# Two edits to the norms of a two-layer encoder: the first norm's small operations on POOL, the last layer's norm by column halves

## The chip, the cores and the metric

One core of a Trainium2 chip runs the whole program. The metric is the device time of one execution in microseconds (us). The core's engines run side by side, each with its own instruction queue worked off in order: PE (matrix products), DVE (vector operations), ACT (activations, with sums along a row), POOL (further vector operations) and SP, whose queue issues the DMA transfers. An engine waits at the head of its queue for semaphores of other engines.

## The reference

Two layers over 1024 positions of width 1024: a recurrent mixer in the first, windowed attention in the second, each followed by an MLP. Each of the four sub-layers is normed before and after:

```
def rmsnorm(x, g):
    xf = x.astype(jnp.float32)
    y = xf * lax.rsqrt(jnp.mean(xf * xf, axis=-1, keepdims=True) + EPS) * g.astype(jnp.float32)
    return y.astype(x.dtype)
...
        h = h + rmsnorm(m.astype(h.dtype), g[1])
        m = sqrelu_mlp(rmsnorm(h, g[2]), mlp_w1[layer], mlp_w2[layer])
        h = h + rmsnorm(m.astype(h.dtype), g[3])
```

So at the end of a sub-layer stand two norms: that of its output m, added to the residual h, and that of the new h, which feeds the next sub-layer. The last sub-layer has only the first of them.

## The kernel before

All products are split into high and low parts of 32-bit floats, three matmuls for one. A scheduler orders the instructions on each engine from the program's text and its own estimates of their durations; the text gives priority, so one edit can move rows elsewhere.

At the end of a sub-layer the output exists as eight blocks of 128 positions by 1024 columns, `acc[b]`, in SBUF. A block's product is made in two column halves of 512, each in its own bank of PSUM (`g2_block`, matmul at L216). Each half is added into `acc` by DVE (L267 in an output projection, L586 in an MLP) or copied by ACT (L264, blocks 0 to 3 of a projection). Then `add_norm(b)` runs the first norm:

- SP loads the old h into hb (L234).
- POOL multiplies acc by the gain into mg (L236). mg has two buffers in a projection and one in an MLP.
- `rsqrt_neg2` makes the scale r: ACT squares the block and sums along the row (L147; a second row of it reads the sum out into ss), DVE makes the mean plus epsilon (ms, L148), ACT takes the root (L149), DVE the reciprocal y (L150), and two DVE operations refine it: e (L151) and r (L152), a Newton step with a factor of -2 that the gains' factor of -0.5 undoes. All of these but the square are 128x1. In profile and order the tiles ss, ms and sq are called a, m and s.
- DVE makes the new h, hb = mg * r + hb (L238), and SP stores it (L243).

`normed` (L183 to L185) repeats `rsqrt_neg2` on hb, and DVE writes hb * r * g over acc at L185. `turn(b)` transposes the result on PE (L191), ACT copies the high part (L204) and DVE subtracts to the low part xl (L205). The last layer's MLP has no second norm and no transposes; there a rule puts block b's L238 behind the adds of block b + 1.

Four such tails run: the two output projections (at about 470 to 550 us and 1520 to 1590 us of the span), the first MLP (1122 to 1190) and the last (2164 to the end). Behind a projection's tail the first products of the MLP (L413) follow, with many DVE operations that prepare their operands (L402 to L406, L356 to L359, L86).

Of the kernel before, what the change touches and what calls it, by code (L numbers as in the profile page):

```python
# [18 lines left out]
P = 128  # L19
D = 1024  # L20
# [31 lines left out]
def trunk_kernel(ctx, tc, x, norm_g, rec_w_in, rec_conv_w, rec_conv_b, rg_w_r, rg_b_r, rg_w_i,  # L52
# [87 lines left out]
    def rsqrt_neg2(pool, src, tag, junk=None):  # L140
        def small(t):
            return pool.tile([P, 1], F32, tag=tag + t, name=t, bufs=3)

        if junk is None:
            junk = pool.tile([P, D], BF16, tag="junk", name="junk", bufs=1)
        ss, ms, sq, y, e, r = (small(t) for t in "amsyer")
        A.activation(junk, src, AF.Square, accum_out=ss)  # L147
        V.tensor_scalar(ms, ss, 1.0 / D, EPS, op0=ALU.mult, op1=ALU.add)  # L148
        mm_state["sqrt"] = A.activation(sq, ms, AF.Sqrt)  # L149
        V.reciprocal(y, sq)  # L150
        V.scalar_tensor_tensor(e, y, ms[:, 0:1], y, op0=ALU.mult, op1=ALU.mult)  # L151
        V.scalar_tensor_tensor(r, e, -3.0, y, op0=ALU.add, op1=ALU.mult)  # L152
        return r
# [20 lines left out]
                if self.strassen:  # L174
                    self.f[i][sh] = x_tile(f"xf{i}{sh}", F32)

    def load_g(pool, layer, j):
        g = pool.tile([P, D], F32, tag="g", name="g", bufs=2)
        Y.dma_start(g, norm_g[layer, j, :].partition_broadcast(P))
        V.tensor_scalar(g, g, -0.5, None, op0=ALU.mult)  # L180
        return g
# [40 lines left out]
    def make_tail(pool, acc, h_src, h_dst, layer, j_post, nxt, nbuf, mb):  # L222


        g_post = load_g(pool, layer, j_post)
        state = {}
        if nxt is not None:
            state["g"] = load_g(pool, *nxt)
            state["xt"] = Acts(nxt[1] == 2)

        def add_norm(b, after):
            m = acc[b]
            hb = pool.tile([P, D], F32, tag="hb", name="hb", bufs=nbuf)
            Y.dma_start(hb, h_src[b * P:(b + 1) * P, :])  # L234
            mg = pool.tile([P, D], F32, tag="mg", name="mg", bufs=mb)
            G.tensor_tensor(mg, m, g_post, op=ALU.mult)  # L236
            r = rsqrt_neg2(pool, m, "rt")
            ins = V.scalar_tensor_tensor(hb, mg, r[:, 0:1], hb, op0=ALU.mult, op1=ALU.add)  # L238
            if after is not None and nxt is None:
                tc.add_manual_dep(ins.ins, after.ins.name,  # L240
                                  mybir.DependencyInfo(mybir.DependencyClass.NoSync, mybir.DependencyReason.DATA),
                                  reason="evacuate the next block first")
            Y.dma_start(h_dst[b * P:(b + 1) * P, :], hb)  # L243
            if nxt is not None:
                normed(pool, hb, state["g"], m)

        def turn(b):
            if nxt is not None:
                prep(acc[b], state["xt"], b)
        return add_norm, turn, state  # L250
# [58 lines left out]
    def mlp(xt, hgs, layer, h_src, h_dst, nxt, pre):  # L309
# [391 lines left out]
        with phase("mlp2", reuse_waits="tile") as pool:  # L701
            seq, fetch, prep, group, finish = strassen_out(pool)
            tiles = {}
            hids = {j: plain_hid(j, hl_tile(xp, "x")) for j in (0, 1)}
            for j in (0, 1):
                split_in_place(*hids[j])
                tiles[j] = hids[j], plain_w2(j, hl_tile(wp, "w1", bufs=3))
            fetch(0)
            fetch(1)
            acc += [yp.tile([P, D], F32, tag="y", name=f"acc{b}") for b in range(NB)]  # L710
            todo = {1: lambda: prep(0), 3: lambda: prep(1)}
            plain((0, 1), tiles, True, None, lambda b: todo.get(b, lambda: None)())
# [618 lines left out]
```

## Time and profile before

| | us |
|---|---|
| median of 3 runs | 2219.73 (2218.73 to 2221.28) |
| the profiled execution | 2219.73 |
| its span | 2218.0 |
| L236, POOL's product, 32 times | 80.3, mean 2.509 |
| ACT's root, 128x1 (L149, for example at 2210.30) | 0.20 |
| DVE add of a half block (L586), median | 0.684 |
| a store of a half megabyte to out, issue to landing, median | 2.6 |

The span is what the profile's records cover. In the timeline's rows the start and the duration of an instruction stand first, then engine, line, operation and the tiles written and read; in brackets how long its engine was idle before it and what ended the wait. "x2" merges two neighbours of one kind. In the stretches' table the busy times of PE, PEld (the weight load), DVE, ACT and POOL follow the length, each with a count, then PE's granted clock, the DMA engines' busy share and GB/s.

### The profile page before, as it was taken

The page shows a single profiled execution, that of the slowest core. Times are in us where ns is not written, and L with a number is a line of the kernel's source. Part 1 is how long each engine was busy: PE and PEld are TensorE (multiplying, and loading weights), DVE is VectorE, ACT ScalarE, POOL GpSimd, SP SyncE. Part 2 cuts the span into 40 slices and gives each one's busy share as a digit, 9 for nine tenths or more (in the row PEclk, how much of TensorE's full clock was granted, in tenths as well). Part 3 has the DMA queues.
Part 4 walks back from the last instruction along what each step waited for, and adds up shares of the span by engine and source line. Part 5 has one row for each costly group of instructions (what it writes and reads, how often), then busy time and mean ns, then how long its engine had stood idle before and what let it go on. Part 6 is the DMA issues. An engine that isn't in the chain of part 4 may idle for free.

```text
span 2218.0 us, 28007 instructions
## 1 busy us (share of the span) xinstructions
PE 2157.0 (97%) x10392; PEld 1781.6 (80%) x10392; DVE 1658.2 (75%) x2731; ACT 1143.9 (52%) x1782; POOL 225.9 (10%) x160
## 2 busy tenths in 40 slices
PE   8989999999999999999999999999999999999998
PEld 7878888787788888888888777777788888888886
DVE  6597867857976665778887776876896665678887
ACT  6566555635654446333444765765654455533332
POOL 0131000002000000000023245311200000000003
PEclk9999999999999999999999999999999999999999
DMA  5201011133444437444344112104354444634443
GB/s 144 62 29 53 29 39 39 39 117 136 144 160 156 153 132 255 153 149 157 114 143 129 43 38 66 37 25 139 127 171 157 145 153 162 222 138 145 156 128 124
DMA packets 179610, 260.87 MB, mean 118 GB/s; under 512 B 16913, under 2 KB 98833, under 8 KB 179473
## 3 DMA queue, kind: packets, MB, share of 16 engines
q1 hardware_dynamic: 179472, 259.07, 35.6%
q8 instruction: 82, 1.34, 0.3%
q14 instruction: 56, 0.45, 0.1%
HBM read 180.92 MB, written 70.78 MB: 113 GB/s over the span
## 4 chain that ended last, share of the span: by engine, by line
PE 78%; DVE 12%; ACT 5%; issue 2%; DMA 1%; POOL 1%; SPq 0%; DVEq 0%; ACTq 0%; POOLq 0%
PE m L413 14%; PE m L116 13%; PE m L677 13%; PE aux L413 10%; PE aux L677 10%; PE m L216 9%; PE aux L1203 1%; PE aux L1198 1%; DVE hb L238 1%; DVE w1hl L86 1%; PE m L1184 1%; PE m L1185 1%; DVE acc L185 1%; ACT sm L1192 1%; PE aux L1025 1%
## 5 line engine op out<-in xcount | busy, mean ns | idle before, releaser
L116 PE MATMUL m<-xh,w1hl 128*128 128x512 f32 (+1 forms) x1472 | 425.7, 369 | 0.0
L116 PEld LDWEIGHTS m<-xh,w1hl 128*128 128x128 f32 x1472 | 266.6, 192 | 38.1 <-ACT xh L204 0.2
L116 PE MATMUL m<-xl,w1hl 128*128 128x512 f32 (+1 forms) x736 | 272.1, 370 | 0.5 <-DVE xl L205 0.5
L236 POOL TENSOR_TENSOR mg<-acc,g 128x1024 f32<-128x1024 f32 x32 | 80.3, 2509 | 1622.6 <-DVE acc L586 1193.9
L86 DVE TENSOR_TENSOR w1hl<-raw,w1hl 128x1024 fp32r<-128x1024 f32 x110 | 138.1, 1257 | 90.7 <-ACT w1hl L85 90.5
L413 PE MATMUL m<-xh,ws 128*128 128x512 f32 x512 | 168.6, 392 | 4.4 <-ACT ws L85 3.0
L413 PE MATMUL aux<-xh,w1hl 128*128 128x512 f32 x512 | 168.7, 391 | 1.8 <-ACT u L429 1.4
L413 PE MATMUL m<-xh,w1hl 128*128 128x512 f32 x512 | 167.0, 389 | 0.0
L600 ACT ACTIVATE hidh<-hidl 128x1536 fp32r<-128x1536 f32 (+1 forms) x56 | 89.4, 1596 | 145.8 <-DMA hidl<-hs 145.8
L677 PE MATMUL m<-w2h,hidh 128*128 128x512 f32 x416 | 161.8, 389 | 0.0
L677 PE MATMUL m<-w2l,hidh 128*128 128x512 f32 x416 | 161.8, 389 | 0.0
L677 PE MATMUL m<-w2h,hidl 128*128 128x512 f32 x416 | 161.8, 389 | 0.0
L116 PEld LDWEIGHTS m<-xl,w1hl 128*128 128x128 f32 x736 | 141.2, 192 | 19.1 <-DVE xl L205 0.8
L601 DVE TENSOR_TENSOR hidl<-hidl,hidh 128x1536 fp32r<-128x1536 f32 (+1 forms) x56 | 105.9, 1891 | 54.8 <-ACT hidh L600 54.8
L85 ACT ACTIVATE w1hl<-raw 128x1024 fp32r<-128x1024 f32 x118 | 124.1, 1054 | 36.6 <-DMA raw<-in_mlp_w_dram 12.0
L85 ACT ACTIVATE w2h<-b 128x1536 fp32r<-128x1536 f32 (+1 forms) x48 | 76.7, 1597 | 103.7 <-PE m L677 58.6
L85 ACT ACTIVATE ws<-s 128x512 fp32r<-128x512 f32 x88 | 55.3, 631 | 140.5 <-PE m L413 79.0
L677 PE MATMUL aux<-w2h,hidh 128*128 128x512 f32 x312 | 121.4, 389 | 0.0
L677 PE MATMUL aux<-w2l,hidh 128*128 128x512 f32 x312 | 121.4, 389 | 0.0
L677 PE MATMUL aux<-w2h,hidl 128*128 128x512 f32 x312 | 121.4, 389 | 0.0
L413 PEld LDWEIGHTS m<-xh,ws 128*128 128x128 f32 x512 | 95.8, 188 | 28.6 <-ACT ws L85 5.6
L413 PEld LDWEIGHTS aux<-xh,w1hl 128*128 128x128 f32 x512 | 96.1, 188 | 22.9 <-ACT u L429 2.3
(294 smaller groups left out, 5011.1 us busy)
## 6 DMA issues: line engine op xcount, KB each, us to landing
raw<-in_mlp_w_dram SPq DMA_DIRECT2D x32, 1024.0 KB, 5.6
hidl<-hs SPq DMA_DIRECT2D x42, 768.0 KB, 4.5
hs<-hid SPq DMA_DIRECT2D x104, 256.0 KB, 2.1
b<-in_mlp_w_dram SPq DMA_DIRECT2D x24, 768.0 KB, 4.8
raw<-in_rec_w_in_dram SPq DMA_DIRECT2D x28, 512.0 KB, 3.7
hidl<-hs SPq DMA_DIRECT2D x14, 1024.0 KB, 5.6
hs<-u SPq DMA_DIRECT2D x52, 256.0 KB, 2.0
hres<-hb SPq DMA_DIRECT2D x24, 512.0 KB, 2.8
```

What stands on the lines that cost most here:

```text
L85: A.activation(hi, src, AF.Copy)
L86: (eng or V).tensor_tensor(lo, src, hi, op=ALU.subtract)
L116: T.matmul(o[:, c0:c0 + nw], a[:, k, :], b[k // 4][half][:, k % 4, c0:c0 + nw], start=(n == 0), stop=(n == 3 * KT - 1))
L185: V.scalar_tensor_tensor(hg, hb, r[:, 0:1], g, op0=ALU.mult, op1=ALU.mult)
L216: T.matmul(o, p_[:, b * P:(b + 1) * P], q_[:, c * 512:(c + 1) * 512], start=(n == 0), stop=(n == n3 - 1))
L236: G.tensor_tensor(mg, m, g_post, op=ALU.mult)
L238: ins = V.scalar_tensor_tensor(hb, mg, r[:, 0:1], hb, op0=ALU.mult, op1=ALU.add)
L413: T.matmul(o, a[:, k, :], b[:, k, :], start=(first and n == 0), stop=(n == 11), skip_group_check=not first)
L600: A.activation(h, f32(l), AF.Copy)
L601: V.tensor_tensor(l, f32(l), h, op=ALU.subtract)
L677: T.matmul(o, a_[:, j, sl], b_[:, j, :], start=(not more and n == 0), stop=(n == last), skip_group_check=more)
L1025: T.matmul(o, a_, b_, start=(i == 0), stop=(i == len(terms) - 1))
```

## The change

In the first norm of the first three tails (tag "rt"), the root is taken by ACT straight from the sum, with scale 1/1024 and a tile of epsilons as bias. DVE keeps the reciprocal and hb. ms, e and r go to POOL, behind its product. The second norms stay as they were. The last MLP's tail gets a norm of its own, `add_norm_last`: the square, the product with the gain (now on DVE), the final hb and the store are each done in two column halves; the halves' sums are added by DVE, and ms, e and r stay there. Its mg has two buffers and its gain one.

```
+    eps = cst.tile([P, 1], F32, name="eps")
+    V.memset(eps, EPS)
...
         A.activation(junk, src, AF.Square, accum_out=ss)
+        if tag == "rt":
+            mm_state["sqrt"] = A.activation(sq, ss, AF.Sqrt, scale=1.0 / D, bias=eps)
+            V.reciprocal(y, sq)
+            G.tensor_scalar(ms, ss, 1.0 / D, EPS, op0=ALU.mult, op1=ALU.add)
+            G.tensor_scalar(e, y, y[:, 0:1], ms[:, 0:1], op0=ALU.mult, op1=ALU.mult)
+            G.tensor_scalar(r, e, -3.0, y[:, 0:1], op0=ALU.add, op1=ALU.mult)
+            return r
         V.tensor_scalar(ms, ss, 1.0 / D, EPS, op0=ALU.mult, op1=ALU.add)
...
+        def add_norm_last(b, after):
+
+            m = acc[b]
+            hb = pool.tile([P, D], F32, tag="hb", name="hb", bufs=nbuf)
+            Y.dma_start(hb, h_src[b * P:(b + 1) * P, :])
+            mg = pool.tile([P, D], F32, tag="mg", name="mg", bufs=mb)
...
+            halves = (slice(0, 512), slice(512, 1024))
+            for i, sl in enumerate(halves):
+                A.activation(junk[:, sl], m[:, sl], AF.Square, accum_out=ss[:, i:i + 1])
+                V.tensor_tensor(mg[:, sl], m[:, sl], g_post[:, sl], op=ALU.mult)
+            V.tensor_tensor(ms, ss[:, 0:1], ss[:, 1:2], op=ALU.add)
+            V.tensor_scalar(ms, ms, 1.0 / D, EPS, op0=ALU.mult, op1=ALU.add)
+            A.activation(sq, ms, AF.Sqrt)
+            V.reciprocal(y, sq)
+            V.scalar_tensor_tensor(e, y, ms[:, 0:1], y, op0=ALU.mult, op1=ALU.mult)
+            V.scalar_tensor_tensor(r, e, -3.0, y, op0=ALU.add, op1=ALU.mult)
+            for sl in halves:
+                ins = V.scalar_tensor_tensor(hb[:, sl], mg[:, sl], r[:, 0:1], hb[:, sl], op0=ALU.mult, op1=ALU.add)
...
+                Y.dma_start(h_dst[b * P:(b + 1) * P, sl], hb[:, sl])
+
         def add_norm(b, after):
+            if nxt is None:
+                return add_norm_last(b, after)
...
-            ins = V.scalar_tensor_tensor(hb, mg, r[:, 0:1], hb, op0=ALU.mult, op1=ALU.add)
...
+            V.scalar_tensor_tensor(hb, mg, r[:, 0:1], hb, op0=ALU.mult, op1=ALU.add)
```

The order of the instructions moves with it. DVE before, in the first MLP's tail, from block 3's second half to its hb (acc_7236 is block 0):

```order
L586 TENSOR_TENSOR acc_7239<-m_9177,acc_7239 128x512
L205 TENSOR_TENSOR xl_9146<-aux,xh_9145 128x4x128
L205 TENSOR_TENSOR xl_9148<-aux,xh_9147 128x4x128
L148 TENSOR_SCALAR m<-a 128x1 x2
L586 TENSOR_TENSOR acc_7240<-m_9237,acc_7240 128x512
L150 RECIPROCAL y<-s 128x1 x2
L151 SCALAR_TENSOR_TENSOR e<-y,m 128x1 x2
L152 SCALAR_TENSOR_TENSOR r<-e,y 128x1 x2
L185 SCALAR_TENSOR_TENSOR acc_7238<-hb,r,g 128x1024
L238 SCALAR_TENSOR_TENSOR hb<-mg,r,hb 128x1024
```

The same place now (acc_7238 is block 0; L619 was L586, L214 was L205, L157 to L161 were L148 to L152, L194 was L185; L152 and L276 are the first norm's reciprocal and hb):

```order
L619 TENSOR_TENSOR acc_7241<-m_9179,acc_7241 128x512
L214 TENSOR_TENSOR xl_9148<-aux,xh_9147 128x4x128
L157 TENSOR_SCALAR m<-a 128x1
L214 TENSOR_TENSOR xl_9150<-aux,xh_9149 128x4x128
L159 RECIPROCAL y<-s 128x1
L160 SCALAR_TENSOR_TENSOR e<-y,m 128x1
L161 SCALAR_TENSOR_TENSOR r<-e,y 128x1
L619 TENSOR_TENSOR acc_7242<-m_9239,acc_7242 128x512
L194 SCALAR_TENSOR_TENSOR acc_7240<-hb,r,g 128x1024
L152 RECIPROCAL y<-s 128x1
L276 SCALAR_TENSOR_TENSOR hb<-mg,r,hb 128x1024
```

Before, the two norms' small operations went in pairs ahead of L185; now the second norm's come alone ahead of it, and the first norm's reciprocal stands directly ahead of hb. On POOL, where before one product followed another, the same tail's last two blocks read now:

```order
L274 TENSOR_TENSOR mg<-acc_7244,g 128x1024
L153 TENSOR_SCALAR m<-a 128x1
L154 TENSOR_SCALAR e<-y,m 128x1
L155 TENSOR_SCALAR r<-e,y 128x1
L153 TENSOR_SCALAR m<-a 128x1
L274 TENSOR_TENSOR mg<-acc_7245,g 128x1024
L154 TENSOR_SCALAR e<-y,m 128x1
L155 TENSOR_SCALAR r<-e,y 128x1
```

Three operations follow each product; in the last block ms stands ahead of it. DVE's last rows of the program before, from the last block's two adds on:

```order
L586 TENSOR_TENSOR acc_16170<-m_18216,acc_16170 128x512
L586 TENSOR_TENSOR acc_16170<-m_18230,acc_16170 128x512
L238 SCALAR_TENSOR_TENSOR hb<-mg,r,hb 128x1024
L148 TENSOR_SCALAR m<-a 128x1
L150 RECIPROCAL y<-s 128x1
L151 SCALAR_TENSOR_TENSOR e<-y,m 128x1
L152 SCALAR_TENSOR_TENSOR r<-e,y 128x1
L238 SCALAR_TENSOR_TENSOR hb<-mg,r,hb 128x1024
```

And now, from the last block's second add on (L252 is the product with the gain, L253 adds the sums, L254 is ms, L256 to L258 are y, e and r, L260 is hb):

```order
L619 TENSOR_TENSOR acc_16172<-m_18262,acc_16172 128x512
L260 SCALAR_TENSOR_TENSOR hb<-mg,r,hb 128x512 x2
L252 TENSOR_TENSOR mg<-acc_16172,g 128x512
L253 TENSOR_TENSOR m<-a 128x1
L254 TENSOR_SCALAR m<-m 128x1
L256 RECIPROCAL y<-s 128x1
L257 SCALAR_TENSOR_TENSOR e<-y,m 128x1
L258 SCALAR_TENSOR_TENSOR r<-e,y 128x1
L260 SCALAR_TENSOR_TENSOR hb<-mg,r,hb 128x512 x2
```

The block before still has its hb directly behind the last add, now in halves, and half of the last block's product follows it. PE's rows in the first MLP's tail differ in one place: block 0's transposes stand three matmuls later. In the attention some 400 of PE's rows, with DVE's, ACT's and POOL's, stand in another order, though nothing there is edited.

More of the change, by code (lines that the diff above doesn't have):

```diff
@@ L175, in blocks, with load_g @@
                     self.f[i][sh] = x_tile(f"xf{i}{sh}", F32)
-    def load_g(pool, layer, j):
-        g = pool.tile([P, D], F32, tag="g", name="g", bufs=2)
+    def load_g(pool, layer, j, bufs=2):
+        g = pool.tile([P, D], F32, tag="g", name="g", bufs=bufs)
         Y.dma_start(g, norm_g[layer, j, :].partition_broadcast(P))
@@ L222, in make_tail @@
     def make_tail(pool, acc, h_src, h_dst, layer, j_post, nxt, nbuf, mb):
-        g_post = load_g(pool, layer, j_post)
+        g_post = load_g(pool, layer, j_post, 1 if nxt is None else 2)
         state = {}
@@ L229, in make_tail @@
             state["xt"] = Acts(nxt[1] == 2)
+        def add_norm_last(b, after):
[3 more added lines that the diff above has]
+            mg = pool.tile([P, D], F32, tag="mg", name="mg", bufs=mb)
+            ss, ms, sq, y, e, r = (pool.tile([P, n], F32, tag="rt" + t, name=t, bufs=3)
+                                   for t, n in zip("amsyer", (2, 1, 1, 1, 1, 1)))
+            junk = pool.tile([P, D], BF16, tag="junk", name="junk", bufs=1)
+            halves = (slice(0, 512), slice(512, 1024))
[10 more added lines that the diff above has]
+                ins = V.scalar_tensor_tensor(hb[:, sl], mg[:, sl], r[:, 0:1], hb[:, sl], op0=ALU.mult, op1=ALU.add)
+                if after is not None:
+                    tc.add_manual_dep(ins.ins, after.ins.name,
+                                      mybir.DependencyInfo(mybir.DependencyClass.NoSync, mybir.DependencyReason.DATA),
+                                      reason="evacuate the next block first")
+                Y.dma_start(h_dst[b * P:(b + 1) * P, sl], hb[:, sl])
         def add_norm(b, after):
+            if nxt is None:
+                return add_norm_last(b, after)
             m = acc[b]
@@ L237, in add_norm @@
             r = rsqrt_neg2(pool, m, "rt")
[L238 to L242, printed above, removed]
+            V.scalar_tensor_tensor(hb, mg, r[:, 0:1], hb, op0=ALU.mult, op1=ALU.add)
             Y.dma_start(h_dst[b * P:(b + 1) * P, :], hb)
-            if nxt is not None:
-                normed(pool, hb, state["g"], m)
+            normed(pool, hb, state["g"], m)
         def turn(b):
@@ L712, in mlp @@
             plain((0, 1), tiles, True, None, lambda b: todo.get(b, lambda: None)())
-            add_norm, turn, st = make_tail(pool, acc, h_src, h_dst, layer, 3, nxt, 3, 1)
+            add_norm, turn, st = make_tail(pool, acc, h_src, h_dst, layer, 3, nxt, 3, 2 if nxt is None else 1)
             js = [2 * p + e for p in last_pairs for e in range(2)]
```

## The prediction

> **What bounds the kernel now.** I read the totals first, then the chain that ended last, then busy time by stretches around the four norm tails.
>
> ```profile
> span 2218.0 us, 28007 instructions
> PE 2157.0 (97%) x10392; PEld 1781.6 (80%) x10392; DVE 1658.2 (75%) x2731; ACT 1143.9 (52%) x1782; POOL 225.9 (10%) x160
> PE 78%; DVE 12%; ACT 5%; issue 2%; DMA 1%; POOL 1%; SPq 0%; DVEq 0%; ACTq 0%; POOLq 0%
> 510.00:582.00 72.00, 66.23 (x314) 52.49 (x313) 64.10 (x106) 44.27 (x78) 13.78 (x5) 1.00 0.29 101
> 1130.00:1190.00 60.00, 57.06 (x318) 48.78 (x318) 51.80 (x113) 31.00 (x67) 20.25 (x10) 0.97 0.45 158
> 1260.00:1450.00 190.00, 180.78 (x939) 142.44 (x939) 141.28 (x363) 126.44 (x289) 77.59 (x71) 0.99 0.18 49
> 1557.00:1620.00 63.00, 58.00 (x278) 45.98 (x277) 60.12 (x101) 40.09 (x74) 11.40 (x4) 1.00 0.29 101
> ```
>
> PE is busy in 97% of the span, so only its idle time can be won. After the stretch, its length and PE's, PEld's, DVE's, ACT's and POOL's busy time stand in each row. The last four blocks of the two output projections leave PE idle for 5.77 and 5.00 us (72.00 - 66.23, 63.00 - 58.00) while DVE is nearly full; the tail of the first MLP leaves 2.94. The fourth tail, the last MLP's, ends the program, and PE's last matmul stands 10 us ahead of its end. Those 24 us less what the end must keep are the change's ground. The attention stretch (9.22 us of idle) isn't edited, but its order moves.
>
> **A wait that fills no queue.** DVE rows of one element can last 2.4 us:
>
> ```profile
> 526.90 2.40 POOL L236 TENSOR_TENSOR mg<-acc,g 128x1024 f32<-128x1024 f32 x1 [4.43 <-DVE e L151]
> 526.91 2.40 DVE L152 SCALAR_TENSOR_TENSOR r<-e,y 128x1 f32<-128x1 f32 x1
> ...
> 535.35 1.27 DVE L238 SCALAR_TENSOR_TENSOR hb<-mg,r,hb 128x1024 f32<-128x1024 f32 x1
> 535.57 3.30 POOL L236 TENSOR_TENSOR mg<-acc,g 128x1024 f32<-128x1024 f32 x1 [6.27 <-DVE acc L267]
> ```
>
> r starts just behind POOL's product and ends with it. In the second pair DVE was first, and the product took 3.30 instead of 2.40: 0.9 more, about what hb still had to run. So a DVE operation with two tensors in SBUF and a POOL operation exclude each other, and the earlier one wins. [...] It speaks against the change as much as for it: DVE gives up e and r, but POOL gets three more readers per block that L185 can shut out.
>
> **First norm on POOL: prices.** In 24 blocks (three tails) DVE loses ms, e and r, and POOL gains three 128x1 operations behind its product. No POOL operation with scalars from a tile is in the trace. The nearest rows are the 128x4 copy and the hand-overs:
>
> ```profile
> L1180 POOL COPY sm<-nsink x32: 183/190/629, 1191.8 to 1498.8; 128x4 f32<-128x4 f32 x32
> 1193.75 1.80 POOL L1110 TENSOR_TENSOR rot<-rot,sin 128x512 f32<-128x512 f32 x1 [1.66 <-DMA rot<-qf]
> 1195.59 0.69 DVE L1111 TENSOR_TENSOR qf<-qf,rot 128x512 f32<-128x512 f32 x1 [1.19 <-POOL rot L1110]
> ```
>
> I take 0.19 (the median) for each, 0.06 between two that depend, 0.04 from POOL to DVE (1193.75 + 1.80 to 1195.59) and 0.07 from DVE to POOL (below: hb ends at 2210.04, the product that waited for it starts at 2210.11). The bounds are nothing, if DVE has other work ahead, and 0.63 each (the copy's slowest row). From y's end to hb that is 0.07 + 0.19 + 0.06 + 0.19 + 0.04 = 0.55 us. On DVE the same way takes 0.51 at the end of the run (y ends at 2210.70, and without the lock's 1.5 us hb would start at 2211.2). So the latency is equal; only the engine differs. It pays where DVE does something else meanwhile. The order shows hb directly behind y in most blocks: DVE stands still for those 0.55 us, and everything queued behind hb with it. What is won is ms (0.08 to 0.15 of DVE time) and the lock where it hit the first norm. The root straight from the sum takes away one hop to DVE and back, about 0.4 us, hidden by the 2.4 us product.
>
> **First MLP's tail.**
>
> ```profile
> 1137.50 1.28 DVE L185 SCALAR_TENSOR_TENSOR acc<-hb,r,g 128x1024 f32<-128x1024 f32 x1
> 1138.83 1.09 PE L191 MATMUL aux<-ident,acc 128*128 128x128 f32 x8 [0.25 <-DVE acc L185]
> 1138.95 1.28 DVE L238 SCALAR_TENSOR_TENSOR hb<-mg,r,hb 128x1024 f32<-128x1024 f32 x1
> ...
> 1159.94 0.68 DVE L586 TENSOR_TENSOR acc<-m,acc 128x512 f32<-128x512 f32 x1
> 1160.77 2.42 POOL L236 TENSOR_TENSOR mg<-acc,g 128x1024 f32<-128x1024 f32 x1 [4.19 <-DVE acc L586]
> 1162.82 0.15 DVE L148 TENSOR_SCALAR m<-a 128x1 f32<-128x1 f32 x1 [0.88 <-ACT junk L147]
> 1163.68 0.35 DVE L151 SCALAR_TENSOR_TENSOR e<-y,m 128x1 f32<-128x1 f32 x2
> 1164.14 1.28 DVE L185 SCALAR_TENSOR_TENSOR acc<-hb,r,g 128x1024 f32<-128x1024 f32 x1
> 1165.34 1.28 DVE L238 SCALAR_TENSOR_TENSOR hb<-mg,r,hb 128x1024 f32<-128x1024 f32 x1
> 1165.57 1.06 PE L191 MATMUL aux<-ident,acc 128*128 128x128 f32 x8
> 1166.53 0.68 DVE L586 TENSOR_TENSOR acc<-m,acc 128x512 f32<-128x512 f32 x1
> ```
>
> A block takes DVE 6.59 us here (1159.94 to 1166.53), in step with PE, whose transposes start 0.15 us behind L185's end: no slack. DVE idles 0.88 us for ACT's sum, and by then the product is over (1163.19), so both e's pass freely. In the new order ms of the first norm is gone, so the second norm's e comes at about 1162.2 and is held by the product until 1163.2: the idle time becomes a lock. Then r (0.3), the add (0.60), L185 (1.20), y (0.15), 0.55 of standing, hb (1.20). With 3.25 us from add to product's end that makes 3.25 + 0.3 + 0.60 + 1.20 + 0.15 + 0.55 + 1.20 = 7.25, with small overlaps 7.1: 0.5 us per block more, on the path. That holds for blocks 2 to 6, five times: +2.5. Block 1's hb now stands ahead of block 0's L185 (before behind it), which puts that L185 about 2 us later while PE has only three more matmuls (0.7) to fill; some 0.8 stays on DVE. In block 6 an xl covers the round trip and hb comes 0.3 earlier. Sum: 2.5 + 0.8 - 0.3 = **+3.0 us**. Bounds: -0.5 (all covered) and +6 (0.63 per POOL operation).
>
> **Output projections.**
>
> ```profile
> 529.41 1.28 DVE L238 SCALAR_TENSOR_TENSOR hb<-mg,r,hb 128x1024 f32<-128x1024 f32 x1
> 541.28 1.27 DVE L238 SCALAR_TENSOR_TENSOR hb<-mg,r,hb 128x1024 f32<-128x1024 f32 x1
> 549.42 1.28 DVE L185 SCALAR_TENSOR_TENSOR acc<-hb,r,g 128x1024 f32<-128x1024 f32 x1
> ```
>
> Block 4's hb, late by the 2.40 of the locked r, comes at about 526.3: 3 us won. Then a block takes 6.5 us instead of 5.93 (541.28 - 529.41 is two), since L185 starts ahead of POOL's e, locks it out for its 1.28, and hb waits 0.6 behind it; the second norm's e also meets the product. Twice 0.6 is given back. Block 7's product now starts later against hb, its e and r follow it, and hb is about 0.8 later than 545.08, but block 6's L185 was moved ahead of it. The last L185 starts at about 549.0, against 549.42. What PE needs next is DVE's full list to 581, so 0.4 to 0.5 comes through: **-0.5 us** in each of the two. Bounds: -3 (DVE's lost 0.5 per block and the lock all kept) and +2.
>
> **The last layer by halves.** The product goes from POOL to two DVE operations, so no lock is left.
>
> ```profile
> 2208.15 0.69 DVE L586 TENSOR_TENSOR acc<-m,acc 128x512 f32<-128x512 f32 x1 [0.27 <-PE m L216]
> 2208.76 1.28 DVE L238 SCALAR_TENSOR_TENSOR hb<-mg,r,hb 128x1024 f32<-128x1024 f32 x1
> 2208.93 1.06 ACT L147 ACTIVATE junk<-acc 128x1024 bf16<-128x1024 f32 x1 [3.87 <-DVE acc L586]
> 2210.11 2.34 POOL L236 TENSOR_TENSOR mg<-acc,g 128x1024 f32<-128x1024 f32 x1 [3.06 <-DVE hb L238]
> 2210.12 0.15 DVE L148 TENSOR_SCALAR m<-a 128x1 f32<-128x1 f32 x1
> 2210.30 0.20 ACT L149 ACTIVATE s<-m 128x1 f32<-128x1 f32 x1 [0.22 <-DVE m L148]
> 2210.54 0.16 DVE L150 RECIPROCAL y<-s 128x1 f32<-128x1 f32 x1 [0.27 <-ACT s L149]
> 2210.74 1.73 DVE L151 SCALAR_TENSOR_TENSOR e<-y,m 128x1 f32<-128x1 f32 x1
> 2212.50 0.16 DVE L152 SCALAR_TENSOR_TENSOR r<-e,y 128x1 f32<-128x1 f32 x1
> 2212.75 1.29 DVE L238 SCALAR_TENSOR_TENSOR hb<-mg,r,hb 128x1024 f32<-128x1024 f32 x1
> ...
> hs<-u SPq DMA_DIRECT2D x52, 256.0 KB, 2.0
> ...
> DMA to landing us min/median/max: 2.6/2.6/3.2
> ```
>
> The add at 2208.15 stays, PE's last matmul sets it. Behind it in the new order: block 6's hb in two halves and the second half of the product, each 0.60 (an add of that size frees DVE after 0.61), to 2210.56. The sum was complete by 2210.1 with a whole square, so it is hidden. Adding the halves and ms 0.38, root and reciprocal 0.43 (2210.12 to 2210.54), e 0.20, r 0.25, and 0.25 to hb: 2211.88; the second hb ends at 2213.16, against 2214.04: -0.9. The last store is 256 KB instead of 512, which lands in 2.0 instead of 2.6: -0.6. Sum **-1.5 us**, bounds -2.2 and -0.5. In the seven blocks before, two more 0.60 on DVE stand against some 1.5 of lock (1.73 less the usual 0.2), so PE isn't held up there.
>
> **Sum.** +3.0 - 0.5 - 0.5 - 1.5 = +0.5 us. The reordered attention I set at 0, with ±4 as its bound (under half of its 9.22 idle, either way). The profiled execution took 2219.73, 1.73 above its span and equal to the median, so the forecast is **2220.2 us**.
>
> **Rivals.** (a) Slower: POOL's operations with two scalars per partition cost more than a copy. Each 0.1 adds 0.2 per hb that stands on the path, some 12 of them, 2.4 us; from 0.35 us each on the sum passes +4.4. At 0.5: +7, 2227. The copy's slow row (0.629) speaks for it, its median against. (b) Faster: e and r really leave DVE, because POOL finishes them under DVE's other work, and the lock of 2.40 stays gone: -2.5 in each projection, 0 in the MLP's tail, -1.5 at the end: 2213.2. DVE at 64.10 of 72.00 speaks for it, hb directly behind y against. (c) The attention's new order alone decides by 3 us or more.
>
> **Chances.** The forecast's case (all within 4.4 us of before) 0.50, (a) 0.22, (b) 0.18, (c) 0.10, half of it inside and the rest split 0.03 slower, 0.02 faster. A measurement can tell about 0.2% (4.4 us): faster 0.20, same 0.55, slower 0.25. The range, 2214.0 to 2226.5, reaches into (a) and (b) and leaves out the far half of each, 0.2 together.
>
> **What would show it.** Right: in the first MLP's tail blocks of about 7.1 us and PE waiting for L185 before transposes; hb 0.5 us behind y; no 2.4 us r; the last hb ending 5.0 us behind the start of the last add (5.9 before). Wrong: POOL's 128x1 rows over 0.35 us, or blocks under 6.6 us there, or a changed idle time of PE in the attention.

## The result and the profile after

The changed kernel took 2237.28 us (median of 4 runs, 2235.22 to 2240.21) against 2219.89 for the kernel before, a ratio of 1.0081 with a 95% interval of 1.0068 to 1.0093: **17.4 us slower**. The forecast was 2220.2, at most 2226.5. The profiled execution took 2240.21, 3 us above the median, so its stages add up to 20.5 us and not to 17.4.

The totals and the shares of the chain that ended last, from the page of the changed kernel:

```profile
span 2238.5 us, 28034 instructions
PE 2163.8 (97%) x10392; PEld 1786.8 (80%) x10392; DVE 1641.3 (73%) x2692; ACT 1147.2 (51%) x1798; POOL 229.7 (10%) x224
PE 78%; DVE 10%; ACT 6%; issue 2%; POOL 2%; DMA 1%; SPq 0%; DVEq 0%; POOLq 0%; ACTq 0%
```

DVE is busy for 17 us less, POOL for 4 us more, and the program is 20 us longer. PE's busy time is 6.8 us longer with the same number of matmuls, at a lower clock (0.992 over the span, 0.994 before); the rest of the 20 us is PE waiting. The stretches that the prediction showed, where they now lie and as long as they now last: the first projection, the first MLP's tail, the attention, the second projection (columns as before):

```profile
511.00:586.00 75.00, 68.80 (x319) 55.01 (x318) 60.31 (x92) 43.60 (x78) 17.73 (x20) 0.98 0.30 99
1137.00:1200.00 63.00, 54.27 (x301) 46.08 (x300) 48.26 (x88) 31.08 (x67) 26.45 (x34) 0.98 0.40 139
1271.00:1461.00 190.00, 177.45 (x908) 140.84 (x908) 133.03 (x346) 122.13 (x279) 78.30 (x70) 0.97 0.16 42
1574.00:1640.00 66.00, 59.49 (x278) 47.27 (x277) 55.17 (x87) 40.36 (x73) 15.12 (x18) 0.97 0.28 96
```

PE's idle time in them is 6.2, 8.7, 12.6 and 6.5 us; it was 5.8, 2.9, 9.2 and 5.0. PE's clock, 1.00 in both projections' rows before, is 0.98 and 0.97.

**Where the time went.** The same PE rows stand in both kernels, so the distance between two of them can be compared: a projection's first product (469.34 before, 470.59 after), the last transposes of its tail, the first MLP's long run of matmuls (852.68, 859.28), the last transposes of the first MLP's tail (1186.68, 1197.66), the second projection's first product (1516.38, 1532.93), the second MLP's long run (1894.86, 1917.23), the last add (2208.15, 2230.23). "Blocks" is the way from a projection's start to its last transposes, "behind" from there to the MLP's long run. The table holds the differences to the kernel before in us, one profiled execution each, for the changed kernel and for the experiments of the next section. It leaves out the time ahead of the first projection (+1.3 for the changed kernel) and the second MLP's long run (-0.3). Stages whose PE rows stand in the same order differ by up to 1.6 between executions (1.4 in the attention of `halves`, 1.6 ahead of the first projection in root_ts1), so a single entry of that size shows nothing by itself. "Blocks" and "behind" are best read together: where a tail ends sooner, PE can wait longer behind it.

| kernel | ratio to before | blocks 1 | behind 1 | MLP's tail | attention | blocks 2 | behind 2 | end |
|---|---|---|---|---|---|---|---|---|
| changed | 1.0081 | +3.2 | +2.2 | +4.4 | +5.6 | +4.1 | +1.8 | -1.6 |
| halves | 0.9999 | 0.0 | 0.0 | -0.5 | +1.4 | -0.5 | -0.1 | -1.6 |
| proj_pool | 1.0054 | +2.5 | +2.2 | 0.0 | +0.1 | +4.0 | +1.9 | -1.6 |
| mlp_pool | 1.0033 | -0.7 | 0.0 | +4.5 | +1.8 | -0.5 | -0.2 | -1.3 |
| pool_only | 1.0091 | +2.6 | +2.2 | +4.3 | +2.9 | +3.8 | +2.0 | -0.4 |
| no_newton | 1.0015 | -3.2 | +3.8 | -1.1 | +2.3 | -2.7 | +3.7 | -1.6 |
| e_twice | 1.010 (one run) | +4.0 | +2.3 | +7.1 | +0.4 | +6.4 | +2.4 | -1.6 |
| early_y | 1.0049 | +0.8 | +3.7 | +2.6 | -0.3 | +2.4 | +3.5 | -1.6 |
| after_ops | 1.0092 | +1.3 | +4.1 | +5.7 | +2.1 | +2.2 | +5.2 | -1.6 |
| root_dve | 0.9991 | -0.3 | +0.1 | -0.3 | +0.7 | +1.2 | -0.2 | -1.4 |
| late_xl | 1.0029 | -0.8 | +4.9 | 0.0 | -0.5 | -1.8 | +4.5 | -1.6 |
| both_dve | 1.0055 | +2.6 | +1.8 | -1.0 | +1.4 | +3.8 | +1.2 | -1.3 |
| root_ts1 | 1.0041 | +2.8 | +2.3 | -1.4 | -0.9 | +3.1 | +1.8 | -1.6 |
| ts_only | 1.0008 | -1.3 | +3.0 | -2.4 | -1.6 | +0.7 | +2.5 | -1.6 |
| hyb | 0.9978 | -0.3 | +0.1 | -2.3 | -0.1 | -1.8 | +0.2 | -1.6 |

**The round trip.** A block of the first MLP's tail, from the changed kernel's timeline (L619 the add, L194 what the transposes wait for, L152 y, L154 and L155 POOL's e and r, L276 hb):

```profile
1155.87 0.68 DVE L619 TENSOR_TENSOR acc<-m,acc 128x512 f32<-128x512 f32 x1
1156.63 2.40 POOL L274 TENSOR_TENSOR mg<-acc,g 128x1024 f32<-128x1024 f32 x1 [2.00 <-DVE acc L619]
1158.45 0.60 DVE L160 SCALAR_TENSOR_TENSOR e<-y,m 128x1 f32<-128x1 f32 x1
1159.76 1.27 DVE L194 SCALAR_TENSOR_TENSOR acc<-hb,r,g 128x1024 f32<-128x1024 f32 x1
1160.96 0.15 DVE L152 RECIPROCAL y<-s 128x1 f32<-128x1 f32 x1
1161.28 0.34 POOL L154 TENSOR_SCALAR e<-y,m 128x1 f32<-128x1 f32 x1 [1.97 <-DVE y L152]
1161.73 0.27 POOL L155 TENSOR_SCALAR r<-e,y 128x1 f32<-128x1 f32 x1
1162.03 1.28 DVE L276 SCALAR_TENSOR_TENSOR hb<-mg,r,hb 128x1024 f32<-128x1024 f32 x1 [0.92 <-POOL r L155]
1163.23 0.68 DVE L619 TENSOR_TENSOR acc<-m,acc 128x512 f32<-128x512 f32 x1
```

DVE stands idle for 0.92 ahead of hb: 0.17 from y's end to e, 0.34 for e, 0.11 between, 0.27 for r, 0.03 to hb. Everything behind hb waits with it, and a block takes 7.36 (1155.87 to 1163.23). Such a wait for r stands ahead of all 24 hb of the three tails, 27.0 us of DVE's time in all. In the projections the trip is longer where L194 starts between y and e:

```profile
533.73 0.16 DVE L152 RECIPROCAL y<-s 128x1 f32<-128x1 f32 x1 [0.20 <-ACT s L151]
533.81 1.27 DVE L194 SCALAR_TENSOR_TENSOR acc<-hb,r,g 128x1024 f32<-128x1024 f32 x1
534.07 1.23 POOL L154 TENSOR_SCALAR e<-y,m 128x1 f32<-128x1 f32 x1 [0.47 <-DVE y L152]
535.40 0.27 POOL L155 TENSOR_SCALAR r<-e,y 128x1 f32<-128x1 f32 x1
535.70 1.29 DVE L276 SCALAR_TENSOR_TENSOR hb<-mg,r,hb 128x1024 f32<-128x1024 f32 x1 [0.62 <-POOL r L155]
```

e lasts 1.23 and not 0.34, and ends 0.22 behind L194's end (535.30, 535.08). So it went with all four e that started beside an L194, which reads two tensors in SBUF: 1.23 each, ending 0.21 or 0.22 behind L194, and 0.34 to 0.36 for the other 20. Such keeping out is called the lock here. So 1.2 us of DVE's own work between y and hb hid only 0.30 of the trip (0.62 is left of 0.92).

**Behind the tail** DVE's rows stand in another order. Before, the last xl (DVE's part of the MLP's last operand) came ahead of the last two u:

```profile
582.03 2.28 DVE L86 TENSOR_TENSOR xl<-xf,xh 128x2048 fp32r<-128x2048 f32 x1
...
584.83 0.69 DVE L473 TENSOR_TENSOR u<-m,u 128x512 f32<-128x512 f32 x1
```

Now it comes behind them, and PE waits for it, which it did not before:

```profile
587.84 0.68 DVE L506 TENSOR_TENSOR u<-m,u 128x512 f32<-128x512 f32 x1
...
589.29 0.69 DVE L506 TENSOR_TENSOR u<-m,u 128x512 f32<-128x512 f32 x1
589.90 2.28 DVE L88 TENSOR_TENSOR xl<-xf,xh 128x2048 fp32r<-128x2048 f32 x1
592.24 0.50 PE L446 MATMUL m<-xl,w1hl 128*128 128x512 f32 x1 [1.70 <-DVE xl L88]
```

**The end.** The last add and the last two halves of hb:

```profile
2230.23 0.69 DVE L619 TENSOR_TENSOR acc<-m,acc 128x512 f32<-128x512 f32 x1 [0.47 <-PE m L225]
...
2234.01 1.41 DVE L260 SCALAR_TENSOR_TENSOR hb<-mg,r,hb 128x512 f32<-128x512 f32 x2
```

hb ends 5.19 us behind the last add's start (5.89 before), and the span 8.27 (9.85).

### The profile page after: what moved, and what is told of

The parts are those of the page before. It is cut to its first block, busy times and chain, and to the rows that moved or that the text cites. A ratio compares the mean times of both kernels' runs of the same rounds, so it can differ in the third digit from the quotient of the medians.

```text
span 2238.5 us, 28034 instructions
## 1 busy us (share of the span) xinstructions
PE 2163.8 (97%) x10392; PEld 1786.8 (80%) x10392; DVE 1641.3 (73%) x2692; ACT 1147.2 (51%) x1798; POOL 229.7 (10%) x224
## 4 chain that ended last, share of the span: by engine, by line
PE 78%; DVE 10%; ACT 6%; issue 2%; POOL 2%; DMA 1%; SPq 0%; DVEq 0%; POOLq 0%; ACTq 0%
PE m L446 15%; PE m L118 13%; PE m L710 12%; PE aux L446 11%; PE aux L710 9%; PE m L225 9%; PE aux L1236 1%; DVE hb L276 1%; PE aux L1231 1%; PE m L1217 1%; PE m L1218 1%; PE aux L1058 1%; ACT sm L1225 1%; ACT acc L149 1%; PE aux L979 1%
## 5 line engine op out<-in xcount | busy, mean ns | idle before, releaser
L274 POOL TENSOR_TENSOR mg<-acc,g 128x1024 f32<-128x1024 f32 x24 | 59.4, 2473 | 967.5 <-DVE acc L619 596.9
```

## The experiments

All kernels but `pool_only` have the last layer by halves. Unless an edit says otherwise, it is made to the changed kernel. Ratios are to runs of the kernel before on the same chip.

### Which edit, which stage

**halves**: the first norms as before.

```
-        if tag == "rt":
-            ...
```

> Only the last layer's norm by column halves; the first norms as before, and the order of the rows ahead of the last tail is that of before. The profile of the changed kernel is 22.4 us late at the second MLP's long matmul runs and 20.5 at its end, so the halves seem to win 1.9 us. Theory (the whole loss is in the other edit): 2219.9 - 1.9 = 2218.0, and the last hb ends about 0.9 us less behind the last add than before. Rival (the 1.9 is only the difference between two executions): 2219.9, no change.

0.9999 (0.9990 to 1.0008). The profile's end is 1.6 us shorter, as in the changed kernel; by the times alone this can't be told from nothing, and the attention of this execution gave 1.4 back. The loss is in the other edit.

**proj_pool** and **mlp_pool**: POOL's ms, e and r in the projections alone, and in the first MLP's tail alone (`ntail` counts the tails; `mlp_pool` has == 1).

```
-        if tag == "rt":
+        if tag == "rt" and ntail["n"] != 1:
```

> POOL's ms, e and r in the two output projections only; first MLP's tail with the norm of before, last layer by halves. PE's order in the attention is then that of before but for 52 rows. By the drift of the changed kernel's profile against before (late by 1.3 at the first tail's start, 6.6 at the first MLP's long runs, 16.6 at the second projection's start, 22.4 at the second MLP's): +5.3 and +5.8 in the projections, nothing in the first MLP's tail and in the attention, -1.9 at the end: 2219.9 + 9.2 = 2229.1. If the attention's order were not what costs there, but POOL's late blocks ahead of it, the attention is at the pace of before here all the same. Rival (the projections cost because a late stage pushes the next): under 2225.

> POOL's ms, e and r in the first MLP's tail only; projections as before, last layer by halves. PE's order in the attention is then that of the changed kernel but for 52 rows. By the drift: +4.3 in the tail (blocks of 7.37 instead of 6.59 us), +5.7 in the attention, -1.9 at the end: 2219.9 + 8.1 = 2228.0. Rival (the attention's loss is an effect of the earlier delays, not of its order): +4.3 - 1.9, 2222.3.

1.0054 (1.0041 to 1.0068) and 1.0033 (1.0021 to 1.0045): 11.1 and 7.3 us by the medians. proj_pool came out as expected; mlp_pool is 3 us below the 2228.0, because its attention lost 1.8 and not the 5.7 of the changed kernel's one execution. Each stage loses where POOL has its operations and nowhere else, but for the attention: its rows aren't edited, it has the changed kernel's order in mlp_pool and loses 1.8, and has that of before in proj_pool and loses nothing.

**pool_only**: the halves undone.

```
-            if nxt is None:
-                return add_norm_last(b, after)
```

> The changed kernel with the last layer's norm as before; PE's order is that of the changed kernel in all rows. If the halves are worth what the profiles show (1.6 us between the last add and the end): the changed kernel plus 1.6, ratio 1.0088. If they are worth nothing: 1.0081. The attention, in the changed kernel's order, shows once more whether it is 2 us or 5.6 us longer than before: if the order costs it is 2 (two other kernels with that order took 1.8 and 2.3) and the rest of the 5.6 was this one execution's clock.

1.0091 (1.0076 to 1.0106); the end is within 0.4 of before again, and the attention is 2.9 longer than before. Of the 5.6 in the changed kernel's one execution, then, some 2 to 3 are the order's.

### The round trip

**no_newton**

```
-            G.tensor_scalar(ms, ss, 1.0 / D, EPS, op0=ALU.mult, op1=ALU.add)
-            G.tensor_scalar(e, y, y[:, 0:1], ms[:, 0:1], op0=ALU.mult, op1=ALU.mult)
-            G.tensor_scalar(r, e, -3.0, y[:, 0:1], op0=ALU.add, op1=ALU.mult)
-            return r
+            return y
```

> The changed kernel with ms, e and r of the first norm left out: hb is scaled by the reciprocal y itself, so the refinement and its factor are missing from the first three tails' results. The order of the other rows is that of the changed kernel but for 30 rows of PE and, beside the 72 rows that are gone from POOL, hardly any elsewhere. Theory 1 (the round trip DVE to POOL to DVE, 0.93 us from y to hb, holds up DVE's queue): the loss in the projections and in the first MLP's tail goes, only the attention's +5.7 and the end's -1.9 stay: 2223.7 or less. Theory 2 (the new order of the rows costs, POOL's latency doesn't): projections stay at +5 each: 2233 or more. Theory 3 (half from each): about 2229.

1.0015 (1.0006 to 1.0024). Theory 1's number. With the same order and no trip, the blocks of the projections are 6.4 and 6.8 us shorter than in the changed kernel (from +3.2 to -3.2, from +4.1 to -2.7) and the MLP's tail 5.5. Part of that is less work: the three operations are gone from DVE and POOL alike. But behind the projections' tails 3.8 and 3.7 are lost in spite of it, which no theory on record had. Blocks and behind together lose 0.6 and 1.0 instead of 5.3 and 5.8. PE's waits behind the first tail are those of the changed kernel (1.9 for xl and 0.2 for u in both); the 1.6 that makes 3.8 out of 2.2 is, by the author's estimate, one stretch at half clock (1.71 in late_xl below), which in the changed kernel lies in the blocks (clock 0.50 from 552.66 to 556.07).

**e_twice**

```
+            G.tensor_scalar(e, e, 1.0, None, op0=ALU.mult)
             G.tensor_scalar(r, e, -3.0, y[:, 0:1], op0=ALU.add, op1=ALU.mult)
```

> The changed kernel with one operation more on POOL in each first norm, e times 1.0, between e and r. In the middle blocks of the first MLP's tail DVE's rows stand in the same order as in the changed kernel. Theory 1 (a block lasts as long as DVE stands behind y): hb follows y by 0.92 + 0.27 + 0.10 = 1.29 us and a block takes 7.37 + 0.37 = 7.74 us. Rival (the block's length is set by the second norm's chain or by PE, and POOL's part is covered): 7.37 still. The attention gets a third order there, so nothing is expected of the whole time but that it is above the changed kernel's if theory 1 holds: 1.010 or more.

Its timeline, the same place of a block (L277 is hb, L620 the add):

```profile
1156.99 0.68 DVE L620 TENSOR_TENSOR acc<-m,acc 128x512 f32<-128x512 f32 x1
...
1163.45 1.29 DVE L277 SCALAR_TENSOR_TENSOR hb<-mg,r,hb 128x1024 f32<-128x1024 f32 x1 [1.22 <-POOL r L156]
1164.65 0.68 DVE L620 TENSOR_TENSOR acc<-m,acc 128x512 f32<-128x512 f32 x1
```

The operation added 0.30 (0.22 and a gap), hb's wait went from 0.92 to 1.22 and the block from 7.36 to 7.66: one for one. 7.74 was expected with a dearer operation. 2241.62 in its one run.

**early_y**

```
+                if tail and b >= 1 and not sl.start:
+                    begin(b - 1)
+                ins = V.tensor_tensor(dst, o, dst, op=ALU.add)
+                ...
+                    tc.add_manual_dep(ins.ins, mm_state["y"].ins.name, ...
```

> The changed kernel with DVE's order alone altered: the first norm of a block is begun in the program's text ahead of the next block's adds, and the next block's first add is held behind the reciprocal y. In the first MLP's tail DVE then has L194, y, add, hb instead of add, L194, y, hb, and in the projections' last blocks y, one or two adds, hb. POOL's rows and their number are the same. The add reads PSUM and only one tensor of SBUF, so POOL isn't shut out. Theory 1 (the loss is the uncovered way from y by POOL to hb): an add of 0.60 fits into the 0.92, so hb waits 0.32 and a block of the first MLP's tail takes 7.37 - 0.60 = 6.77 us; that tail loses 1 instead of 4.4 us, and each projection 2 to 4 less than 5.3 and 5.8. The attention gets a third order, 0 to +3. About 2228 where the changed kernel has 2236. Rival (POOL's operations cost by blocking DVE, not by the wait): blocks of 7.37 still, 2236.

1.0049 (1.0032 to 1.0065): about 7 us less than the changed kernel, near the 2228 expected. Its timeline:

```profile
1158.37 0.15 DVE L152 RECIPROCAL y<-s 128x1 f32<-128x1 f32 x1
1158.45 0.67 DVE L639 TENSOR_TENSOR acc<-m,acc 128x512 f32<-128x512 f32 x1
1159.45 1.29 DVE L287 SCALAR_TENSOR_TENSOR hb<-mg,r,hb 128x1024 f32<-128x1024 f32 x1 [0.33 <-POOL r L155]
...
1165.35 0.67 DVE L639 TENSOR_TENSOR acc<-m,acc 128x512 f32<-128x512 f32 x1
```

0.33 is left of the wait and a block takes 6.90 (6.77 expected). From y's end to hb are 0.93 us with the add between (1158.52 to 1159.45) and 0.92 without: this add, which takes one of its inputs from PSUM, did not hold POOL up, where L194 made 1.23 out of e's 0.34. But this is only a part of the 7 us: the MLP's tail loses 2.6 instead of 4.4 where 1 was expected; the projections' blocks gain 2.4 and 1.7, and give 1.5 and 1.7 back behind; the rest lies in the attention, which has a third order here (-0.3). So the number was met in part by luck.

### The order of the rows

**after_ops**: the last two operands prepared earlier in the text.

```
             V.tensor_tensor(b11, t2, b11, op=ALU.subtract)
+            V.tensor_tensor(b21, b21, t2, op=ALU.subtract)
...
-            V.tensor_tensor(b21, b21, t2, op=ALU.subtract)
-            for p in both:
-                side_by_side(p, 7)
...
             split(*acts[4], b21)
+            for p in both:
+                side_by_side(p, 7)
```

> The changed kernel, and in the MLPs the last two operands are prepared earlier in the program's text (the second xf ahead of the products 6, the last xl ahead of the products 7), so that DVE has xf, xl, hid, xl there as before the change; of PE's rows 52 move, back to their places of before, and no other row of the tails does. Theory A (a projection's loss of about 5.3 us has two parts: 2.5 to 3 in the blocks, where DVE stands behind y for POOL, and 2.2 to 2.9 behind the tail, because the change's new order puts the last xl behind more rows): ratio to before 1.0081 less 5 us, 1.0058, and PE's wait of 1.70 us for that xl at about 592 us is gone. Theory B (DVE is late there only because the tail is): no change against the changed kernel, 1.008.

1.0092 (1.0077 to 1.0106), no gain where theory A had 1.0058. The wait of 1.70 is gone, but the xl before it now comes later, and PE waits 3.04 for that one. By itself this told nothing: the order wasn't brought back to that of before, only changed again.

**root_dve**: ms, e and r on DVE, the root straight from the sum.

```
-            G.tensor_scalar(ms, ss, 1.0 / D, EPS, op0=ALU.mult, op1=ALU.add)
-            G.tensor_scalar(e, ...
-            G.tensor_scalar(r, ...
+            V.tensor_scalar(ms, ss, 1.0 / D, EPS, op0=ALU.mult, op1=ALU.add)
+            V.scalar_tensor_tensor(e, y, ms[:, 0:1], y, op0=ALU.mult, op1=ALU.mult)
+            V.scalar_tensor_tensor(r, e, -3.0, y, op0=ALU.add, op1=ALU.mult)
```

> The changed kernel with ms, e and r of the first norms on DVE again, the root still taken by ACT straight from the sum; last layer by halves. The order of the rows is nearly that of before (20 rows of PE, none of them in the attention). Theory 1 (the loss is POOL's round trip and the order that it brings): all of it is gone, 2217.9 less 0 to 2: 2216 to 2218. Rival (ACT's root with a bias, 0.28 instead of 0.20, and the sum's hand-over cost): above 2220.

0.9991 (0.9981 to 1.0000). The root straight from the sum costs nothing, and with nearly the order of before no stage loses more than 1.2, which is within the difference between executions.

**late_xl**: root_dve, and two rows of DVE held back.

```
-            V.tensor_tensor(b21, b21, t2, op=ALU.subtract)
+            hold(V.tensor_tensor(b21, b21, t2, op=ALU.subtract), (0, 6))
...
-            split(*acts[4], b21)
+            hold(split(*acts[4], b21), (1, 7))
```

> The kernel with ms, e and r on DVE and the root straight from the sum (ratio 0.9991, no loss in the projections), with one thing of the changed kernel's order: in the MLPs DVE's second xf waits for the first hid of the products 6, and the last xl for the second u of the products 7, by an order alone; 88 of PE's rows move. Theory (the order behind the tail costs by itself): PE waits for the last xl by 1 to 2 us at about 585 us, may fall to half its clock for 3.4 us after it, and each MLP's start takes 2 to 4 us longer: ratio 1.001 to 1.003. Rival (that order only shows where the tail is already late): 0.999, and no wait for xl.

1.0029 (1.0020 to 1.0039), some 8 us more than root_dve and inside the range expected. PE's wait in its timeline:

```profile
588.76 0.51 PE L446 MATMUL m<-xl,w1hl 128*128 128x512 f32 x1 [1.70 <-DVE xl L88]
```

And its stretches of 1 us from there on, with PE's clock as the third number from the end:

```profile
588.00:589.00 1.00, 0.23 (x1) 0.24 (x2) 1.00 (x2) 0.00 (x0) 0.00 (x0) 1.00 0.00 0
589.00:590.00 1.00, 1.00 (x4) 0.76 (x4) 0.31 (x1) 0.63 (x1) 0.00 (x0) 0.56 0.12 35
590.00:591.00 1.00, 1.00 (x4) 0.81 (x3) 0.00 (x0) 0.63 (x1) 0.00 (x0) 0.50 0.80 158
591.00:592.00 1.00, 1.00 (x3) 0.77 (x3) 0.00 (x0) 0.00 (x0) 0.00 (x0) 0.50 1.06 370
592.00:593.00 1.00, 1.00 (x5) 0.75 (x4) 0.00 (x0) 0.00 (x0) 0.00 (x0) 0.73 1.08 381
```

So this order alone, with nothing of the norms on POOL but the product, costs 4.9 and 4.5 us behind the two tails, of which 4.0 can be named: a wait of 1.70 for xl, 0.56 for u ahead of it, and 1.71 more from half a clock (1 - clock, summed over the stretches). The blocks ahead, 0.8 and 1.8 shorter than before, give part of it back in this execution. This is the part of a projection's loss that lies behind its tail; from the last xf on, DVE's order is that of the changed kernel, but that xf stands one row earlier.

**both_dve**: the second norms' root straight from the sum too, all on DVE.

```
-        mm_state["sqrt"] = A.activation(sq, ms, AF.Sqrt)
+        mm_state["sqrt"] = A.activation(sq, ss, AF.Sqrt, scale=1.0 / D, bias=eps)
```

> Both norms with the root straight from the sum and all small operations on DVE, so that the second norm's hop from ACT to DVE and back (about 0.4 us) goes too; last layer by halves. The second norm's chain ends in the operation that PE's transposes wait for. If that chain is what sets a block in the first MLP's tail: 0.2 to 0.4 us less per block, 6.59 to 6.3, some 2 us there. PE's order in the attention is that of the changed kernel but for 186 rows in all, and the MLP's operands are in its order as well: +2 there and +2 behind each projection if these orders cost by themselves: 2217.9 + 6 - 2 = 2222. If only POOL's round trip costs and the orders are worth nothing: 2215.

1.0055 (1.0041 to 1.0068), worse than the 2222 expected. The MLP's tail gains 1.0; the projections lose 4.4 and 5.0 with no operation of the norms on POOL but the product. In the first projection's blocks PE waits 3.3 for one xl of the transposes. That another order of the rows costs as much as the trip is the likely reading; here it isn't tried apart from the second norms' root.

### Without the trip and without the lock

**root_ts1** and **ts_only**: e and r with one tensor and two scalars per partition, on DVE; the first norms of root_dve, and all norms of `halves`.

```
-            V.scalar_tensor_tensor(e, y, ms[:, 0:1], y, op0=ALU.mult, op1=ALU.mult)
-            V.scalar_tensor_tensor(r, e, -3.0, y, op0=ALU.add, op1=ALU.mult)
+            V.tensor_scalar(e, y, y[:, 0:1], ms[:, 0:1], op0=ALU.mult, op1=ALU.mult)
+            V.tensor_scalar(r, e, -3.0, y[:, 0:1], op0=ALU.add, op1=ALU.mult)
```

> As the kernel with ms, e and r on DVE and the root straight from the sum (ratio 0.9991), but e and r of the first norms as operations of one tensor with y and ms as scalars per partition, as POOL had them. In the profile of before ms, which has that form, takes 0.15 us beside POOL's product (at 2210.12), while e with two tensors takes 1.73 and r 2.40. Theory (what is shut out is the second tensor in SBUF): first norms' e and r take 0.15 to 0.25 even beside the product, none lasts over 0.6; in each projection 0 to 2.5 us less: ratio 0.997 to 0.999. Rival (scalars from a tile are shut out as well): e or r of 1.7 to 2.4 us remain, ratio 0.999.

> Before's norms on DVE (ms ahead of the root) with e and r of both norms as operations of one tensor with two scalars per partition; last layer by halves. If the form isn't shut out, the second norm's e, 0.35 to 0.6 us in the first MLP's tail of the changed kernel, takes 0.2 as well. The order of 334 of PE's rows differs from before, so the attention may take 0 to 3 us more. Theory: ratio 0.998 to 1.000. Rival (the new order of rows costs as in the kernel with both roots straight from the sum, 1.0055): 1.003 or more.

1.0041 (1.0028 to 1.0053), above the 0.997 to 0.999 expected, and 1.0008 (0.9999 to 1.0017). The form does what was hoped, the whole time doesn't. All executions of e in the kernel before (count, then shortest, median and longest in ns):

```profile
L151 DVE SCALAR_TENSOR_TENSOR e<-y,m x64: 208/220/2394, 7.1 to 2210.7; 128x1 f32<-128x1 f32 x64
```

And in ts_only:

```profile
L153 DVE TENSOR_SCALAR e<-y,m x56: 261/272/277, 7.3 to 1589.7; 128x1 f32<-128x1 f32 x56
```

None of 56 is held up, though 14 of them start inside a POOL product. The MLP's tail gains 2.4, but the projections get another order and lose 5.1 and 4.9 (root_ts1), 1.7 and 3.2 (ts_only).

**hyb**: that form in the first MLP's tail alone, with before's norms there; root_dve in the projections.

```
+        if tag == "rt" and ntail["n"] != 1:
+            ...
+        if ntail["n"] == 1:
+            V.tensor_scalar(e, y, y[:, 0:1], ms[:, 0:1], op0=ALU.mult, op1=ALU.mult)
+            V.tensor_scalar(r, e, -3.0, y[:, 0:1], op0=ALU.add, op1=ALU.mult)
+            return r
```

> All small operations on DVE. Projections as in the kernel with the root straight from the sum (no loss there); in the first MLP's tail the norms of before with e and r as operations of one tensor and two scalars, which the kernel with that form in all tails ran 2.4 us faster than before; last layer by halves. 182 of PE's rows stand in another order than before. If each stage keeps what it had: -2.4 in the first MLP's tail, -1.6 at the end, 0 to +1 in the projections, 0 to -1.5 in the attention: ratio 0.998. If the order of the projections or of the attention moves as in the other kernels: 1.000 or more.

0.9978 (0.9969 to 0.9987): 2214.51 against 2218.96, as expected and 0.2% faster than before. The projections kept their order. In the stretch of the first MLP's tail that the prediction showed, PE is now busy for 59.12 of 60 us (57.06 before):

```profile
1130.00:1190.00 60.00, 59.12 (x348) 51.09 (x347) 50.55 (x114) 31.29 (x68) 21.17 (x10) 1.00 0.47 166
```

## Why the prediction was wrong, step by step

**The price of the trip** was mis-sized. I had 0.55 from y to hb, with 0.19 for each operation on POOL from a 128x4 copy's median. e and r take 0.34 and 0.27, the gap is 0.1, the way there 0.17, the way back 0.03: 0.92. These were inside the bounds that the prediction gave, and rival (a) had the direction; its point of decision, 0.35 each, was nearly reached. It doesn't explain the size: by its own price, 0.37 more for each of "some 12" hb on the path are 4.4 us, or 2224.6. All 24 hb waited for r, 27.0 us in all, and what these waits set off wasn't in it.

**First MLP's tail, +3.0, measured +4.4.** The mechanism was right (DVE stands behind y, L185 is late, PE waits 3.0 us for it where it waited 0.6, the second norm's e is held by the product: 0.60), and only the size was off: blocks of 7.36 to 7.38 and not 7.1, by the missing 0.37 of the trip less small overlaps.

**Output projections, -0.5 each, measured +5.3 and +5.8.** This is the step that failed, in two places. In the blocks the gain of block 4 was there in part: no r of 2.4 us is left, but the hb ahead of it waited 1.27 for r, and of the 3 us foretold 1.7 came (hb at 528.94 instead of 529.41, with a start 1.25 later). The lock by L185 and hb's wait of 0.6 behind it were foretold rightly, yet a block takes 6.8 to 6.9 us (L276 at 528.94 and 535.70) and not 6.5, so the last L194 starts at 553.02 instead of 549.0, of which 1.25 were there at the projection's start.

And "what PE needs next is DVE's full list to 581" took that list as given. It isn't: the scheduler reordered it with the change, the last xl ends 39.2 us behind the last L194 where it was 34.9, and late_xl shows that such an order alone costs 4.5 to 4.9 behind the tail. The orders shown ahead of the prediction stop at the tails; rows of DVE and PE behind them had moved too, and no term priced them. The changed kernel shows only 2 of that behind the tail because its stretch at half clock came earlier, in the blocks: their +3.2 and +4.1 are 1.3 and 2.3 of idle PE and 1.8 of slower matmuls each.

**What a wait costs beyond itself** was in no term. Behind some waits PE ran at half its clock for 3.41 us (0.50 from 552.66 to 556.07), 1.71 us lost each time if PE had work throughout. From 460 us to the last MLP's end I count seven such stretches in the changed kernel's profile (two of them on end, from 1389), four in that of before: up to 5.1 of the 20.5 us. No term of the prediction is about it, though its own row from 1130 to 1190 has a clock of 0.97.

**Attention, 0 with a bound of 4.** The order costs some 2 to 3 (mlp_pool 1.8, no_newton 2.3, pool_only 2.9); in the changed kernel's profile it was 5.6, of which 2.1 were clock. So rival (c) happened in part, and the sign that was named for it, a changed idle time of PE there, came: 9.2 became 12.6. The waits that grew, before and after (total, times, longest):

```profile
PE m L1184 <- DMA kh<-kh: 2.2, 1, 2.2
PE m L1184 <- POOL qst L1138: 1.0, 2, 0.6
```

```profile
PE m L1217 <- DMA kh<-kh: 4.3, 1, 4.3
PE m L1217 <- POOL qst L1171: 3.0, 4, 1.6
PE m L1217 <- DVE nm L1219: 2.2, 1, 2.2
```

Others shrank; in all PE's waits there are 12.7 us before and 16.1 after. That these waits come from the order, and not from delays ahead of it, rests on proj_pool: its attention starts 4.9 us late, in the old order, and loses 0.1. The order wasn't tried alone.

**The last layer, -1.5, measured -1.6** in nearly every profile, and the last hb ends 5.19 behind the add where 5.0 was foretold. The sum was right by some luck: hb gained 0.7 and not 0.9 (the prediction's terms add up to 2212.07 and not to its 2211.88, which makes 0.7), and the way from hb to the end 0.9 and not 0.6. The times can't confirm so small a gain (0.9999, within 0.1%).

**Rival (b)** had a true core: early_y shows that POOL's e and r can be hidden, in these runs under an add that takes something from PSUM (0.33 left of the wait) and hardly under L194 (0.62 left), and the order that the scheduler chose put nothing else between y and hb.

## What to carry to other kernels

Before small operations are moved to another engine, ask what stands between the producer and the consumer on the engine that stays: if nothing, the round trip (0.92 us here) is idle time for the whole queue, and work that shuts the other engine out covers little of it (0.30). Where a scheduler sets the order, an edit's largest cost may lie in rows that it doesn't name: compare the orders behind the edited place too, and price the rows that move in front of what the busiest engine waits for. If one operand form is what gets locked out, change the form before the engine (here e took 0.26 to 0.28 us in the one form and up to 2.39 in the other).

## What the hardware showed

**Half a clock after short waits.** From 460 us to the last MLP's end a stretch at half speed lasted 3.41 us in the changed kernel (clock 0.50 from 552.66 to 556.07, 1.00 from there to 559) and in that of before, or twice that, as from 1388.93 to 1395.76 in the changed kernel. In late_xl PE had 0.56, 0.50, 0.50 and 0.73 of full speed in the last four stretches above, 1.71 us lost. In each of the two traces these stretches start a whole number of such lengths apart (552.66 and 1197.78 in the changed kernel are 189 lengths of 3.413, 1185.78 and 1213.08 in that of before are 8). The same wait of 1.70 for xl was followed by one in late_xl (588.76), and by none in the changed kernel (592.24). What differs between these two is PE's idle time added up over the length ahead: 2.25 us in late_xl (585.72 to 589.13) and 2.01 ahead of the changed kernel's dip at 552.66, where the wait of 1.62 and most of one of 0.61 stand, but 1.70 in the length that holds the wait at 592 (590.21 to 593.62). PE wasn't idle throughout ahead of the two dips: it was busy for 1.16 and 1.40 us of the 3.41. And the idle time alone doesn't tell where a dip follows: in the changed kernel one follows 1.70 of it as well (1225.09 to 1228.50), in the trace of before one follows 1.50 (ahead of 1462.26) and none 1.55 (564.56 to 567.97).

**Scalars weren't locked out.** A DVE operation of 128x1 with its second and third input as scalars per partition took 0.26 to 0.28 us in ts_only, beside POOL's product too (14 rows; in hyb 0.27 at 1161.22, inside a product from 1159.47 to 1162.76), while the one with two tensors took up to 2.39 in the kernel before.

**POOL's small operations** of 128x1, e with two scalars from tiles, r with one, m with constants alone, all 24 of each in the changed kernel (busy time, mean ns; the mean of e holds the four of 1.23 us beside L194, with 0.34 to 0.36 for the rest, and that of m two of 1.04 and 1.06 beside hb, with 0.19 for the rest):

```profile
L154 POOL TENSOR_SCALAR e<-y,m 128x1 f32<-128x1 f32 x24 | 11.8, 492 | 30.4 <-DVE y L152 29.9
L155 POOL TENSOR_SCALAR r<-e,y 128x1 f32<-128x1 f32 x24 | 6.4, 267 | 2.4
L153 POOL TENSOR_SCALAR m<-a 128x1 f32<-128x1 f32 x24 | 6.3, 264 | 7.3 <-ACT junk L149 5.5
```
